# Latents of the attention scaled by 1/rms before their transposes, in a two-layer trunk on one core

## The chip, the core and the metric

The kernel runs on one core of one Trainium2 chip. A core has TensorE (PE, which also loads weights, PEld), VectorE (DVE), ScalarE (ACT), GpSimd (POOL) and SyncE (SP, which here only issues DMAs). Each takes its instructions strictly in the order of its own queue and waits on semaphores for the others. The metric is the device time of one execution in microseconds, less is better.

## What is computed

Two layers of a trunk over 256 tokens of width 1024 in fp32. Each layer is a feed forward, a mixing stage of three branches (a recurrence, a stick-breaking attention, a latent attention) and a second feed forward. The change is in the latent attention, whose queries, keys and values come from two normalized latent vectors of width 256:

```python
def rms_norm(x, g):
    xf = x.astype(jnp.float32)
    y = xf * lax.rsqrt(jnp.mean(xf * xf, axis=-1, keepdims=True) + NORM_EPS)
    return (y * g.astype(jnp.float32)).astype(x.dtype)
...
def mla_branch(c_q_raw, c_kv_raw, k_rope_raw, q_norm, w_uq, kv_norm, w_ukv, cos, sin):
    B, S, _ = c_q_raw.shape
    q = (rms_norm(c_q_raw, q_norm) @ w_uq).reshape(B, S, MLA_HEADS, MLA_NOPE + MLA_ROPE)
    q_nope, q_rope = jnp.split(q, [MLA_NOPE], axis=-1)
    q_rope = apply_rope(q_rope, cos[:, :, None, :], sin[:, :, None, :])
    kv = (rms_norm(c_kv_raw, kv_norm) @ w_ukv).reshape(B, S, MLA_HEADS, MLA_NOPE + MLA_V)
    k_nope, v = jnp.split(kv, [MLA_NOPE], axis=-1)
    k_rope = apply_rope(k_rope_raw, cos, sin)
    ...
    o = chunk_causal_softmax_attention(q, k, v, (MLA_NOPE + MLA_ROPE) ** -0.5)
```

Since 1/rms is one number per token, it can be multiplied onto the latent before `w_uq` and `w_ukv`, or onto what these give.

## The kernel before

**Weights.** All matrices come from HBM as one stream, in the order of use. Two blocks of [128, 512] make a piece. Each piece is split into two float32r parts: ACT casts it to `hi` (128x1024), DVE subtracts to get `lo`. `next_sub` asks for this two pieces ahead of PE (`AHEAD`), and there are four buffers of each part. For each block PE does pairs of matmuls, `hi` against both parts of the activations side by side (128x512) and `lo` against the high part (128x256). A whole piece is 8 such pairs. Activations are split in the same way into tiles `r`; `f` are plain fp32 tiles, `acc` and `side` tiles are PSUM.

**Groups.** The mixing stage is a list of matmul groups, `MIX_ORDER`. `cq` and `ckv` make the latents, with tokens on the partitions. `uq`, `uqr` (from the query latents), `ukv` and `uv` (from the key/value latents) have only two k-tiles; `uq` and `ukv` put features on the partitions and tokens on the free axis, `uqr` and `uv` the reverse. `rgx` and `rgg` belong to the recurrence, `q`, `k`, `v` to the stick-breaking attention, `ga`, `gb`, `gc` are gates, `bra`, `brb`, `brc` multiply the branches' results by their matrices. Of interest are these stretches of the list:

```python
v0 k0 rgx0 rgx1 k1 q0 q1 cq0 q2 q3 k2 rgx2 v1 k3 rgx3 rgg0 rgg1 rgg2 rgg3
gb0 uq0 gb1 uq1 gb2 uq2 gb3 uq3 uqr0 brb0 brb1 ckv0 brb2 brb3 ga0 ukv0 ga1 ukv1 uv0 ga2 ukv2
```

**Side work.** What isn't a group (attention of a pair of heads, the recurrence of a pair of channel blocks in `rg_chain`, latents, gelu) is written as generators. `Tasks` emits their instructions between those of the groups, each generator's in its order, where a `Clock` of estimated times says that they hold up no engine; per step only some 350 ns of side work go to PE. So the order on each queue is fixed when the program is built, by these estimates, and a change in one generator moves the others' instructions too. All that passes through `Tasks` has the line of one helper, L197, in the profile: rows are told apart by tiles.

**The latents.** `latents` evicts a latent from PSUM times 1/rms of the trunk's own norm (tile `rms`), transposes it at once (`transpose_pair`) and splits it, times the gain, into the `r` tile that `Latent` hands to the groups. Behind that, ACT sums squares (`ssc`), POOL makes 1/rms (`rc`, by `rsqrt_mean`: a multiply-add and a power), and `broadcast` turns the two columns into a row on all partitions: DVE multiplies the identity by each column, PE multiplies the diagonals by a matrix of -1, and ACT copies the result to SBUF. `head_T` then multiplies each result of `uq` and `ukv` by that row on DVE (in `scaled`), and `gen_scaled` those of `uqr` and `uv` by the columns as it evicts them.

In `rg_chain` ACT and DVE split the weights and the input of the gates of one channel pair into `r` tiles (128x512), and PE multiplies these (`side<-r,r`). There are four channel pairs.

Of the kernel before, what the change touches and what calls it, by code (L numbers as in the profile page):

```python
# [11 lines left out]
ALU = mybir.AluOpType  # L12
# [11 lines left out]
# columns of the packed per-layer vectors  # L24
# [12 lines left out]
# of each group of columns: the matrix, the first column, the k-tiles  # L37
# [9 lines left out]
def group_stream(what, n):  # L47
    """Sub-blocks of [128, 512]: one k-tile of 512 columns, or two k-tiles of 256."""
# [17 lines left out]
def layer_stream(l):  # L66
    """Order in which a layer's weight sub-blocks of [128, 512] are read."""
# [22 lines left out]
class Slots:  # L90
    """Tiles handed out in the order in which they were given back."""
# [17 lines left out]
# for each function the tables to load for it; a table holds all functions that name it  # L109
# [10 lines left out]
class Clock:  # L120
    """Estimated times (ns): until when each engine is held by what has been emitted, and
    when each tile's contents are there and have been read."""
# [33 lines left out]
class Op:  # L156
    """An instruction to be emitted, with what it costs by the clock."""
# [42 lines left out]
class Timed:  # L200
    """An engine whose instructions are emitted at once from the main stream, and left to
    the scheduler from side work."""
# [15 lines left out]
class Tasks:  # L218
    """Side work: generators whose instructions are emitted, each generator's in order, where
    the clock says that they hold up no engine. What follows a yield runs after what came  # L220
    before it has been emitted."""
# [57 lines left out]
    def advance(self, t, force=False):  # L279
        """Emits what it can of a task; whether there was any."""  # L280
# [32 lines left out]
    def drain(self, *tasks, done=None):  # L313
        """Emits the given tasks, whether they fit or not, to their end or until `done`."""
# [19 lines left out]
def trunk(tc, xT_in, pos_in, w_in, rgw_in, fin_in, const_in, out):  # L334
# [4 lines left out]
    with ctx:  # L339
# [18 lines left out]
        # x^T, two k-tiles of [128, 256] in each  # L358
# [4 lines left out]
        # [hi | lo] of two k-tiles  # L363
# [27 lines left out]
        def load(out, in_):  # L391
            """One of the first loads: they come one after the other."""
            nc.sync.dma_start(out=out, in_=in_)  # L393
            n = 4 * 128
            for d in out.shape[1:]:
                n *= d
            arrival[0] += max(n / 360, 475)
            clock.written[out.tensor.name] = (arrival[0] + 950, "dma")
# [56 lines left out]
        def both(ap):  # L455
            """[128, 256] as [128, 2, 256]"""
            return ap.rearrange("p (j t) -> p j t", j=1).to_broadcast([128, 2, 256])

        def hilo(src, hl, j=None, g=1.0):
            """src [128, 2, 256], or k-tile j of it, in two float32r parts."""  # L460
# [39 lines left out]
        def parts(a):  # L500
            """What of [128, 2, ...] each tile of a's holds."""
# [7 lines left out]
        def feature_group(kts, evac, last=0):  # L509
            """256 features of all tokens: the two halves of a bank are summed by `evac`. The  # L510
            last steps run block by block."""
# [18 lines left out]
        def token_group(kts, evac, last=0):  # L530
            """512 features, tokens on the partitions."""
# [15 lines left out]
        def narrow_group(kts, width, weights, evac):  # L547
            """The same with [128, width] weights, as (hi, lo) from `weights`."""
# [9 lines left out]
        def features(a):  # L558
            """What a feature group made, to SBUF."""
# [8 lines left out]
        def scaled(a, src, key, extra=None):  # L568
            """The same, times a scale per token."""
            f = yield from features(a)  # L570
            while key not in src:
                yield 1
# [10 lines left out]
        def transpose_pair(srcs, o):  # L583
            """Two [128, 128] blocks from column o of every token tile, to [128, 2, 256]."""
# [18 lines left out]
        def first_norm(nm, n):  # L603
            """K-tiles 2n and 2n+1 of x are final: their two parts, and squares."""
# [37 lines left out]
        def broadcast(b, r, dst, key, start=False):  # L642
            """Columns r [128, NT], to a row of them on every partition."""
# [819 lines left out]
```

## Time and profile before

| what | value |
|---|---|
| time, three runs | 1466.5, 1467.37, 1467.78 us |
| median | 1467.37 us |
| span of the profiled execution | 1467.2 us |
| PE busy | 1442.0 us (98%) |
| DVE busy | 1115.6 us (76%) |
| ACT busy | 894.3 us (61%) |
| POOL busy | 146.1 us (10%) |
| chain that ended last | PE 92%, DVE 5%, issue 1%, ACT 1% |

The span runs from the first to the last instruction of one execution; the times are of whole runs without a profiler. An engine counts as busy while one of its instructions runs, waits on a semaphore are idle. PE's matmuls overlap in the records, so the length of one row isn't what it costs: that is read from start to start. The granted clock of TensorE was 0.999 of full speed over the span.

### The profile page before, as it was taken

The numbers are of one execution on the slowest core, as the hardware profiler recorded it, in microseconds if no ns is written. First come the engines' busy times: TensorE is split into PE (matmuls) and PEld (weight loads), VectorE is DVE, ScalarE is ACT, GpSimd is POOL, SyncE is SP. The second block draws the span as 40 slices with busy tenths as digits, with TensorE's granted clock in tenths as the row PEclk, the third lists the DMA queues.
The fourth block names the chain that finished last, engine by engine and source line by source line (L and its number), as shares of the span: only waits on it lengthen the run. The fifth ranks groups of instructions, "written<-read, shape, count | busy, mean of one in ns | idle before, by whom it ended". The sixth has DMA issues, their size and how long they took to land.

```text
span 1467.2 us, 20804 instructions
## 1 busy us (share of the span) xinstructions
PE 1442.0 (98%) x8248; PEld 1261.0 (86%) x8248; DVE 1115.6 (76%) x1548; ACT 894.3 (61%) x1372; POOL 146.1 (10%) x120
## 2 busy tenths in 40 slices
PE   6999999999999999999999999999999999999998
PEld 5888888888888888888888888898888888888886
DVE  6878567689987788877677766676989877877853
ACT  4665446888665656665455554478885655566643
POOL 3000001123310000000000000111334000100001
PEclk9999999999999999999999999999999999999999
DMA  6555555534543455555545554544445434555452
GB/s 215 199 201 177 197 180 180 179 134 153 182 171 144 145 199 176 197 188 187 200 172 189 184 200 173 187 174 149 151 156 189 169 122 173 195 190 196 179 199 86
DMA packets 38081, 258.15 MB, mean 176 GB/s; under 512 B 4320, under 2 KB 4960, under 8 KB 7520
## 3 DMA queue, kind: packets, MB, share of 16 engines
q1 hardware_dynamic: 37152, 254.21, 48.5%
q0 software_dynamic: 832, 2.62, 0.6%
q8 instruction: 64, 1.05, 0.3%
q14 instruction: 33, 0.27, 0.1%
HBM read 255.77 MB, written 1.05 MB: 175 GB/s over the span
## 4 chain that ended last, share of the span: by engine, by line
PE 92%; DVE 5%; issue 1%; ACT 1%; DMA 0%; SPq 0%; POOLq 0%; POOL 0%; DVEq 0%; ACTq 0%
PE acc L197 77%; PE side L197 15%; DVE lo L197 2%; DVE f L197 2%; DVE r L197 1%; DMA x<-xT 0%; ACT hi L197 0%; ACT f L197 0%; SPq L393 0%; ACT r L197 0%; POOLq L1459 0%; POOL rms L197 0%; DVE rms L197 0%; DVEq L197 0%; ACTq L197 0%
## 5 line engine op out<-in xcount | busy, mean ns | idle before, releaser
L197 PE MATMUL acc<-r,hi 128*128 128x512 f32 x3148 | 1135.1, 403 | 9.4 <-ACT hi L197 5.5
L197 PE MATMUL acc<-r,lo 128*128 128x256 f32 x3148 | 882.7, 280 | 2.1 <-DVE lo L197 2.1
L197 DVE TENSOR_TENSOR lo<-raw,hi 128x1024 fp32r<-128x1024 f32 (+2 forms) x485 | 596.4, 1232 | 235.7 <-ACT hi L197 234.2
L197 PEld LDWEIGHTS acc<-r,hi 128*128 128x128 f32 x3148 | 593.0, 188 | 141.0 <-ACT hi L197 5.5
L197 PEld LDWEIGHTS acc<-r,lo 128*128 128x128 f32 x3148 | 596.7, 190 | 5.6 <-DVE lo L197 3.1
L197 ACT CAST hi<-raw 128x1024 fp32r<-128x1024 f32 (+2 forms) x485 | 501.5, 1040 | 137.3 <-PE acc L197 95.0
L197 POOL TENSOR_TENSOR f<-f,f 128x512 f32<-128x512 f32 (+1 forms) x51 | 89.1, 1753 | 1039.8 <-ACT f L197 955.8
L197 ACT COPY f<-acc 128x512 f32<-128x512 f32 x166 | 97.4, 587 | 126.7 <-PE acc L197 122.9
L197 ACT ACTIVATE f<-f 128x256 f32<-128x256 f32 (+3 forms) x190 | 94.9, 502 | 84.5 <-DVE f L197 83.3
L197 DVE TENSOR_TENSOR f<-acc,f 128x512 f32<-128x512 f32 x166 | 113.8, 685 | 39.1 <-ACT f L197 38.5
L197 DVE TENSOR_TENSOR f<-f,f 128x512 f32<-128x512 f32 x179 | 126.3, 706 | 8.8 <-ACT f L197 2.6
L197 PE MATMUL acc<-hi,r 128*128 128x512 f32 (+2 forms) x344 | 96.9, 358 | 0.0
L197 ACT CAST r<-f 128x256 fp32r<-128x256 f32 (+2 forms) x130 | 58.6, 455 | 61.1 <-DVE f L197 59.8
L197 PE MATMUL side<-r,hi 128*128 128x512 f32 x260 | 92.0, 395 | 0.0
L197 PE MATMUL side<-r,lo 128*128 128x256 f32 x260 | 72.6, 279 | 0.0
L197 PE MATMUL side<-f,f 128*128 128x256 f32 (+1 forms) x320 | 71.6, 327 | 0.0
L197 PEld LDWEIGHTS acc<-hi,r 128*128 128x128 f32 x344 | 61.6, 189 | 8.4
L197 DVE TENSOR_TENSOR r<-f,r 128x256 fp32r<-128x256 f32 (+2 forms) x130 | 64.7, 502 | 2.0 <-ACT r L197 1.9
L197 PE MATMUL acc<-lo,r 128*128 128x512 f32 (+2 forms) x172 | 61.1, 355 | 0.0
L197 PEld LDWEIGHTS side<-r,hi 128*128 128x128 f32 x260 | 48.7, 187 | 11.1
L197 PEld LDWEIGHTS side<-f,f 128*128 128x128 f32 x320 | 45.8, 190 | 4.9
L197 PEld LDWEIGHTS side<-r,lo 128*128 128x128 f32 x260 | 49.1, 189 | 0.0
(89 smaller groups left out, 806.2 us busy)
## 6 DMA issues: line engine op xcount, KB each, us to landing
raw<-w SPq DMA_DIRECT2D x238, 1024.0 KB, 4.8
f<-rgw POOLq DMA_DIRECT2D x8, 256.0 KB, 3.4
raw<-w SPq DMA_DIRECT2D x7, 256.0 KB, 6.9
out<-f SPq DMA_DIRECT2D x4, 256.0 KB, 2.2
x<-xT SPq DMA_DIRECT2D x3, 256.0 KB, 6.7
f<-fin POOLq DMA_DIRECT2D x2, 256.0 KB, 3.7
cst<-const SPq DMA_DIRECT2D x1, 336.0 KB, 5.5
x<-xT SPq DMA_DIRECT2D x2, 128.0 KB, 2.5
```

The costliest lines, as they stand in the source:

```text
L197: return self.f(*self.args, **self.kw)
```

## The change

The squares, the mean and the power of a latent now come before its transposes, and DVE multiplies the two token tiles of the latent by 1/rms in place, in SBUF. What `uq`, `uqr`, `ukv` and `uv` give is then normalized already: `head_T` skips the product, `gen_scaled` copies, and the broadcast of the row is gone, with the tiles that held it. Comments and docstrings are dropped as well.

```diff
         def scaled(a, src, key, extra=None):
             f = yield from features(a)
+            if key is None:
+                return f
             while key not in src:
                 yield 1
             rb = both(src[key])
...
-        def broadcast(b, r, dst, key, start=False):
+        def broadcast(b, r, dst, key):
...
-            pe.matmul(b[:, 256:512], neg_one, d[:, 0:256], start=start, stop=True, skip_group_check=True)
+            pe.matmul(b[:, 256:512], neg_one, d[:, 0:256], start=False, stop=True, skip_group_check=True)
...
-        def gen_scaled(a, scales):
+        def gen_scaled(a, scales=None):
             o = []
             for t in range(NT):
                 f = yield from FT.take()
-                if t == 0:
+                if scales is None:
+                    act.copy(f, bank_of(a, t)) if t == 0 else dve.tensor_copy(f, bank_of(a, t))
+                elif t == 0:
                     act.activation(out=f, in_=bank_of(a, t), func=AF.Copy, scale=scales[t])
...
             def run(a):
-                f = yield from scaled(a, mx["nm"] if r == "rb" else mx, r, extra)
+                f = yield from scaled(a, mx["nm"], r, extra)
...
                 yield
                 acc.give(a)
                 cs_ = [c[:, t * 256:(t + 1) * 256] for t in range(NT)]
+                junk = yield from FT.take()
+                for t in range(NT):
+                    act.activation(out=junk[:, 0:256], in_=cs_[t], func=AF.Square, accum_out=mx["ssc"][:, i, t:t + 1])
+                yield
+                FT.give(junk)
+                rsqrt_mean(mx["rc"][:, i], mx["ssc"][:, i], 256)
+                for t in range(NT):
+                    dve.tensor_scalar(cs_[t], cs_[t], mx["rc"][:, i, t:t + 1], None, op0=ALU.mult)
                 yield
                 b = yield from transpose_pair(cs_, 0)
                 hl = yield from RT.take()
...
                 side.give(b)
+                FT.give(c)
                 mx["cT"][i] = hl
-                yield
-                junk = yield from FT.take()
-                for t in range(NT):
-                    act.activation(out=junk[:, 0:256], in_=cs_[t], func=AF.Square, accum_out=mx["ssc"][:, i, t:t + 1])
-                yield
-                FT.give(junk, c)
-                rsqrt_mean(mx["rc"][:, i], mx["ssc"][:, i], 256)
-                yield
-                b = yield from side.take()
-                yield from broadcast(b, mx["rc"][:, i], mx, ("rbq", "rbkv")[i], start=True)
                 if i == 1:
                     yield from k_rope(mx, f)
...
                 elif what == "uq":
-                    feature_group(Latent(0), head_T(mx, "qn", n, "rbq"))
+                    feature_group(Latent(0), head_T(mx, "qn", n, None))
...
                 elif what == "ukv":
-                    feature_group(Latent(1), head_T(mx, "kn", n, "rbkv"))
+                    feature_group(Latent(1), head_T(mx, "kn", n, None))
                 elif what == "uv":
-                    token_group(Latent(1), head_v(mx, "v_ml", n, mx["rkv"]))
+                    token_group(Latent(1), head_v(mx, "v_ml", n, None))
```

The order of the built program shows where instructions land. Numbers behind a tile's name tell buffers apart and differ between the two programs.

DVE, first layer, around the key/value latents, before: the eviction of the latent (`f_120<-acc_84,rms`), the two low parts behind the transposes (`r_100<-side_87,cst`), and the diagonals made from `rc`.

```order
L197 TENSOR_SCALAR f_120<-acc_84,rms_171 128x256
L197 SCALAR_TENSOR_TENSOR f_113<-f_122,f_133 128x256 x2
L197 TENSOR_TENSOR lo<-raw,hi 128x1024
L197 SCALAR_TENSOR_TENSOR r_100<-side_87,cst,r_100 128x256
L197 TENSOR_TENSOR f_110<-f_125,cs 128x8x32
L197 SCALAR_TENSOR_TENSOR f_119<-f_132,f_119 128x512
L197 SCALAR_TENSOR_TENSOR r_100<-side_87,cst,r_100 128x256
L197 TENSOR_TENSOR f_110<-f_110,f_138 128x8x32
L197 TENSOR_TENSOR lo<-raw,hi 128x1024
L197 TENSOR_SCALAR f_118<-cst,rc_1815 128x128 x2
L197 TENSOR_TENSOR f_115<-acc_85,f_115 128x512
```

The same place now: the latent is `f_139`, the low parts are `r_98<-side_89,cst`.

```order
L197 TENSOR_SCALAR f_139<-acc_84,rms_171 128x256
L197 SCALAR_TENSOR_TENSOR f_126<-f_122,f_126 128x512
L197 TENSOR_TENSOR f_137<-f_137,f_121 128x8x32
L197 TENSOR_TENSOR lo<-raw,hi 128x1024
L197 SCALAR_TENSOR_TENSOR r_93<-f_111,r_93 128x2x256
L197 TENSOR_SCALAR f_139<-f_139,rc_1815 128x256 x2
L197 SCALAR_TENSOR_TENSOR f_127<-f_122,f_126 128x256 x2
L197 TENSOR_TENSOR lo<-raw,hi 128x1024
L197 SCALAR_TENSOR_TENSOR r_98<-side_89,cst,r_98 128x256
L197 TENSOR_TENSOR f_128<-acc_85,f_128 128x512
L197 SCALAR_TENSOR_TENSOR f_128<-f_138,f_128 128x512
L197 SCALAR_TENSOR_TENSOR r_98<-side_89,cst,r_98 128x256
```

The scalings (`f_139<-f_139,rc`) stand ahead of the low parts, and the two diagonals behind them are gone. Behind the last row come the key's rotation (14 instructions of 128x32 and 128x64) and two weight splits. On POOL four products of 128x512 stand directly ahead of `rc`, and the product behind it reads the scans `f_127`.

DVE, first layer, before, where the splits of the third and fourth channel pair end (`r_98` of the third, `r_103` and `r_93` of the fourth).

```order
L197 TENSOR_TENSOR lo<-raw,hi 128x1024
L197 TENSOR_TENSOR f_119<-acc_84,f_119 128x512
L197 TENSOR_TENSOR f_119<-f_119,f_109 128x512
L197 SCALAR_TENSOR_TENSOR f_128<-f_126,f_127 128x256
L197 TENSOR_TENSOR r_98<-f_116,r_98 128x512
L197 TENSOR_TENSOR lo<-raw,hi 128x1024
L197 TENSOR_TENSOR r_103<-f_117,r_103 128x512
L197 TENSOR_TENSOR r_93<-f_118,r_93 128x512
L197 TENSOR_TENSOR r_94<-side_86,r_94 128x2x256
```

And now, some 24 rows earlier, the third pair's (`r_104`, `r_93`), and 21 and 27 rows later, in the second fence, the fourth pair's (`r_103`, `r_96`).

```order
L197 TENSOR_TENSOR lo<-raw,hi 128x1024
L197 SCALAR_TENSOR_TENSOR f_128<-f_126,f_127 128x256
L197 TENSOR_TENSOR r_101<-f_135,r_101 128x384
L197 SCALAR_TENSOR_TENSOR f_128<-f_126,f_127 128x256
L197 TENSOR_TENSOR r_104<-f_138,r_104 128x512
L197 TENSOR_TENSOR r_93<-f_112,r_93 128x512
L197 TENSOR_TENSOR lo<-raw,hi 128x1024
```

```order
L197 TENSOR_TENSOR r_103<-f_141,r_103 128x512
L197 TENSOR_TENSOR lo<-raw,hi 128x1024
L197 TENSOR_TENSOR f_138<-acc_84,f_138 128x512
L197 TENSOR_TENSOR f_138<-f_138,f_109 128x512
L197 TENSOR_TENSOR f_112<-side_86,f_112 128x256
L197 TENSOR_TENSOR lo<-raw,hi 128x1024
L197 TENSOR_TENSOR f_112<-side_89,f_112 128x256
L197 TENSOR_TENSOR r_96<-f_130,r_96 128x512
```

What stood in one run is now in two places, 46 rows and more apart.

ACT, first layer, now, between the gates of the third pair and the scores of a stick-breaking head (`f_113`); the rows from one cast of weights to the second after it.

```order
L197 CAST hi<-raw 128x1024
L197 CAST r_94<-side_86 128x2x256
L197 CAST r_98<-f_117 128x384
L132 ACT_TABLE_LOAD
L197 ACTIVATE f_116<-side_87,cst 128x256
L197 ACTIVATE f_114<-side_87,cst 128x256
L197 ACTIVATE f_115<-f_116,tiny,s_77 128x256
L197 ACTIVATE f_113<-side_88 128x384
L132 ACT_TABLE_LOAD
L197 ACTIVATE f_113<-f_113 128x384
L197 CAST hi<-raw 128x1024
L197 COPY f_139<-acc_84 128x512
```

Behind these follow one more `ACTIVATE f_113<-f_113`, a third table load, one `ACTIVATE f_116<-side_86,cst` and the next cast of weights. The number of table loads in the whole program is 33 in both.

## Rows read from the trace of the kernel before

**Rows 1.** The page: span, PE's busy time, the chain that ended last by engine.

```profile
span 1467.2 us, 20804 instructions
...
PE 1442.0 (98%) x8248; PEld 1261.0 (86%) x8248; DVE 1115.6 (76%) x1548; ACT 894.3 (61%) x1372; POOL 146.1 (10%) x120
...
PE 92%; DVE 5%; issue 1%; ACT 1%; DMA 0%; SPq 0%; POOLq 0%; POOL 0%; DVEq 0%; ACTq 0%
```

**Rows 2.** Waits of PE: who waited for whom, us in total, times, longest.

```profile
PE side L197 <- DVE r L197: 4.7, 4, 1.5
...
PE side L197 <- DVE f L197: 1.9, 2, 0.9
```

**Rows 3.** Timeline of PE at the gates: start, length, instruction, idle before.

```profile
340.48 0.38 PE L197 MATMUL side<-r,r 128*128 128x256 f32 x1 [0.90 <-DVE r L197]
...
344.32 0.62 PE L197 MATMUL side<-r,r 128*128 128x256 f32 x3 [1.47 <-DVE r L197]
```

**Rows 4.** Timeline of DVE and POOL at the same moments.

```profile
340.35 1.63 DVE L197 TENSOR_TENSOR lo<-raw,hi 128x1024 fp32r<-128x1024 f32 x1
341.90 2.37 DVE L197 TENSOR_TENSOR r<-f,r 128x512 fp32r<-128x512 f32 x2
...
340.99 2.13 POOL L197 TENSOR_TENSOR f<-f,f 128x512 f32<-128x512 f32 x1
```

**Rows 5.** Timeline of PE around the broadcast of the query latents, first layer.

```profile
268.36 0.39 PE L197 MATMUL acc<-r,hi 128*128 128x512 f32 x1
...
268.71 0.39 PE L197 MATMUL acc<-r,hi 128*128 128x512 f32 x1
...
269.05 0.59 PE L197 MATMUL side<-f,cst 128*128 128x256 f32 x2
...
269.83 0.40 PE L197 MATMUL acc<-r,hi 128*128 128x512 f32 x1
```

**Rows 6.** Timeline of POOL, DVE and PE around the broadcast of the key/value latents.

```profile
404.18 0.19 POOL L197 TENSOR_SCALAR rc<-ssc 128x2 f32<-128x2 f32 x1 [10.85 <-ACT f L197]
404.45 0.72 POOL L197 TENSOR_TENSOR rc<-rc,nhalf 128x2 f32<-128x2 f32 x1
...
405.15 2.28 POOL L197 TENSOR_TENSOR f<-f,f 128x512 f32<-128x512 f32 x1
...
406.21 1.83 DVE L197 TENSOR_SCALAR f<-cst,rc 128x128 f32<-128x128 f32 x2
...
408.10 0.70 PE L197 MATMUL side<-f,cst 128*128 128x256 f32 x2 [0.93 <-DVE f L197]
```

**Rows 7.** Instructions on the tile `rc`: shortest, median and longest, in ns.

```profile
L197 DVE TENSOR_SCALAR f<-cst,rc x8: 278/444/1772, 267.2 to 1129.8; 128x128 f32<-128x128 f32 x8
```

**Rows 8.** Groups by shape, PE and DVE: count, busy us, mean ns, idle before.

```profile
L197 PE MATMUL side<-f,cst 128*128 128x256 f32 x20 | 6.1, 388 | 1.9 <-DVE f L197 1.9
...
L197 DVE TENSOR_TENSOR lo<-raw,hi 128x1024 fp32r<-128x1024 f32 x476 | 590.4, 1242 | 232.5 <-ACT hi L197 230.9 <-PE side L197 0.3
L197 DVE TENSOR_TENSOR f<-f,f 128x512 f32<-128x512 f32 x171 | 122.9, 719 | 8.6 <-ACT f L197 2.6
...
L197 DVE TENSOR_TENSOR_SCAN f<-f,f 128x256 f32<-128x256 f32 x16 | 11.3, 723 | 0.0
...
L197 DVE TENSOR_TENSOR r<-f,r 128x512 fp32r<-128x512 f32 x22 | 16.8, 780 | 0.0
...
L197 DVE TENSOR_SCALAR f<-f,sm 128x256 f32<-128x256 f32 x16 | 5.5, 346 | 0.0
...
L197 DVE TENSOR_TENSOR f<-f,cs 128x32 f32<-128x32 f32 x16 | 2.0, 184 | 0.0
```

**Rows 9.** Groups by shape, ACT.

```profile
L197 ACT CAST hi<-raw 128x1024 fp32r<-128x1024 f32 x476 | 497.0, 1049 | 133.7 <-PE acc L197 95.0 <-PE side L197 25.7 <-issue 7.3
...
L132 ACT ACT_TABLE_LOAD x33 | 42.3, 1283 | 1.3 <-PEq L1455 0.7
...
L197 ACT ACTIVATE f<-side,cst 128x256 f32<-128x256 f32 x32 | 14.6, 474 | 6.2 <-PE side L197 6.1
```

More of the change, by code (lines that the diff above doesn't have):

```diff
@@ L1014, in run @@
             def run(a):
-                qs = yield from gen_scaled(a, mx["rq"])
+                qs = yield from gen_scaled(a)
                 yield
@@ L1149, in mix @@
             mx["rc"] = pool.tile([128, 2, NT], F32, name=f"rc{l}")
-            mx["rq"] = [mx["rc"][:, 0, t:t + 1] for t in range(NT)]
-            mx["rkv"] = [mx["rc"][:, 1, t:t + 1] for t in range(NT)]
             mx["sm"] = pool.tile([128, 3, HEADS, NT], F32, name=f"sm{l}")
@@ L1292, in mix @@
                     RT.give(*nm["xT"].values())
-            FT.give(nm["rb tile"], mx["rbq tile"], mx["rbkv tile"])
+            FT.give(nm["rb tile"])
             FT.give(mx["kr"])
```

## The prediction

> **What bounds the kernel now.** I read the page's head first: of a span of 1467.2 us TensorE (PE) is busy for 1442.0 us, 98%, and the chain that ended last lies on PE for 92% and on VectorE (DVE) for 5% [rows 1]. So work taken from DVE, ScalarE (ACT) or GpSimd (POOL) is worth nothing by itself. Worth something are only PE's own instructions and the moments at which PE stands still.
>
> Those moments are in the list of what PE waited for [rows 2]. Two kinds lie in the mixing stage: waits of `side` matmuls for DVE's `r` tiles, 4.7 us in 4 times, and for DVE's `f` tiles, 1.9 us in 2 times. They come at the same places in both layers, half of them in each. PE's other idle time is nearly all at the kernel's start, which the change doesn't touch.
>
> The timeline of the first layer tells what they are. At 340.48 and 344.32 us gate matmuls of the recurrence (`side<-r,r`) waited 0.90 and 1.47 us for the low part of their input [rows 3]. DVE wasn't idle then but behind: it had a weight split and two such splits in a row, and while POOL worked on a product of 2.13 us the weight split took 1.63 us and the two others together 2.37 us [rows 4]; by the means of their kinds that would be 1.24 and 1.56 us [rows 8]. The wait for an `f` tile is the row of 1/rms of the key/value latents: the broadcast matmul at 408.10 stood in PE's queue 0.93 us for the diagonals that DVE makes from `rc`, and the two instructions that make them took 1.83 us [rows 6].
>
> **The change, part by part.** *PE loses four fp32 matmuls*, one broadcast per latent and layer; they are 8 of the 20 records `side<-f,cst` of 128x256 [rows 8], each matmul being recorded as two. Their price is read where one stood with no wait: from 268.71 to 269.83 PE did two pairs of weight matmuls (high and low part) and one broadcast in 1.12 us, and the pair before them took 0.35 us, 268.36 to 268.71 [rows 5]. So 1.12 - 0.70 = 0.42 us each, 4 x 0.42 = 1.7 us. Nothing covers these, PE being the chain.
>
> *The wait ahead of the key/value broadcast goes with it*: 1.9 us for both layers [rows 2].
>
> *DVE loses* 16 products of 128x512 (`f<-f,f`, 8 per layer) of 0.72 us [rows 8] and 8 diagonal instructions of 0.44 us in the median [rows 7], and gets 8 scalings of 128x256 inside SBUF. The trace has that operation and shape on another tile, `f<-f,sm`, at 0.35 us [rows 8]. That is 11.5 + 3.5 - 2.8 = 12 us less. The six copies that replace a scaling per token out of PSUM cost about what those did, and ACT loses four copies of the broadcast. I price all this at nothing: PE's 98% covers it, and if DVE were the bound where these stood, it would be up to 12 us, of which the trace shows no more than the waits already named. Squares, mean and power are as many as before, only ahead of the transposes.
>
> *What moves.* The scheduler decides by estimated times, so from the first latent on nearly every side instruction stands elsewhere. The order shows what becomes of the 4.7 us. Before, the last low splits of the third and fourth channel pair stood together on DVE with one weight split between them. Now the third pair's two come some 25 rows earlier, and the fourth pair's stand two weight splits apart and some 25 rows later. The pile for which PE waited is gone, and I take the whole 4.7 us off. Its bounds are that and nothing, if the pile has only moved.
>
> *What the moves may add.* Two places look tight in the new order, each once per layer.
>
> First, the key/value latents. Behind the last ckv matmul DVE has up to the weight split that follows the scalings: two weight splits of 1.24 us, a product of 0.72, the two scalings of 0.35, two scans of 0.72 [rows 8], together 5.3 us, and an eviction, a rotation and a split of about 0.5 us each, so 7 us. Then come the two low parts of the latents, an eviction with its product and the key's rotation in 14 instructions of some 0.18 us [rows 8], another 5 us, and only then the weight split that PE needs four weight pieces after ckv. A piece is 8 pairs of 0.35 us, so 11.2 us, and a dozen transposes add about 1.3 us. That split is done after 7 + 5 + 1.2 = 13.2 us and wanted after 12.5: 0.7 us late. Should POOL hold DVE up once more, as at 406.21, where 1.83 us went into two instructions that take 0.28 us at best [rows 6, 7], it is 1.3 us more, 2.0 in all. The least is nothing.
>
> Second, ACT has three table loads close together, with a single cast of weights among them. Up to the second cast that is 3 x 1.28 for the loads, 2 x 1.04 for the casts and ten smaller instructions of about half a us [rows 9], 11 us for two pieces, while PE uses up two pieces in 5.6 us. The weights are split two pieces ahead, 5.6 us of lead. The two amounts are nearly equal; I take 0.8 us late, with bounds of nothing and of 2.8 us, if the lead was one piece only.
>
> Together 2 x (0.7 + 0.8) = 3.0 us, between nothing and 2 x (2.0 + 2.8) = 9.6 us. That the latents are ready later costs nothing by itself: twelve groups of matmuls lie between cq and its first use, and brb2, brb3 and ga0 between ckv and its own.
>
> **The sum** against the profiled span: 1467.2 - 1.7 - 1.9 - 4.7 + 3.0 = 1461.9 us. The median of the three runs, 1467.4, is 0.2 us above that span, so 1462 us.
>
> **A row against the change.** The diagonal's instructions, with one input and both ends in SBUF as the new scalings have them, took 0.28 us at least, 0.44 in the median and 1.77 at most, all of one shape [rows 7]; the slow pair ran while POOL multiplied for 2.28 us [rows 6]. So the change keeps the exposure that made the broadcast late. If POOL multiplies at one scaling of each latent, it costs DVE 4 x (1.83 - 2 x 0.28) = 5 us, and the sum is 1467 us if PE waits for all of it.
> The Trainium skill's page "SBUF — State Buffer", section "Who interferes with whom", says that such an instruction of VectorE and one of GpSimd exclude each other on a shared pair of ports for its whole length, so that the second to issue waits; the trace agrees at 406.21.
> I don't add these 5 us, since for the key/value latents POOL's next product reads the scans that DVE makes behind the scalings and can't run beside them; it is a rival.
>
> **The rivals.** A time is told from the 1467.4 us of before when it differs by more than 0.2%, 2.9 us: under 1464.4 or over 1470.3.
> *No new waits*: 8.3 us gained, 1459 us. For it speaks that PE shows hardly a wait at the other tight places of the old order; against it the two sums above. 20%.
> *The waits come back elsewhere*: the two tight places cost over 5.5 us in all, or a gate pile re-forms: 1466 us, no change. For it speaks that DVE and ACT are still full there. 17%.
> *POOL holds up the scalings*, as worked out above: 1467 us, no change. For it speaks the pair at 406.21, against it what POOL's next product reads. 6%.
> *Slower*: POOL is late with the power. In the new order four products of 128x512, of 2.1 to 2.3 us each in the rows seen [rows 4, 6], stand on POOL right ahead of the mean and the power, where it was idle for 10.85 us before [rows 6]. If they start only when ckv ends, the power is there 4 x 2.1 + 0.9 = 9.3 us behind it. DVE, which takes its instructions in order and is there after some 3.5 us, stands still for 5.8 us with the weight splits queued behind, and PE waits for those: 2 x 5.8 us on top of the forecast, 1473 us. It decides from 4.2 us per layer, a power 7.7 us behind ckv. Against it: most of the four products have their inputs some pieces earlier. 5%.
> *The forecast*: 52%.
>
> **Numbers.** 1462 us. The range runs from no new waits, 1458.5, to waits that come back nearly whole, 1467.0. Faster 0.71 (nearly all of the forecast and of no new waits), same 0.24, slower 0.05.
>
> **What would show it.** Right: 12 records `side<-f,cst` of 128x256 are left, PE's list has no wait for an `f` tile in the mixing stage and under 1 us per layer for `r` tiles; DVE is busy some 12 us less and PE some 1.7 us less. Wrong: PE waits of over 2 us per layer for `lo` behind ckv, for `hi` near the three loads, or for the latents' transposes with POOL named behind DVE. The forecast falls too if the gate splits are late again, now for the third pair alone, which would return 2 to 5 us.

## The result, and the profile after

The changed kernel takes 1477.96 us (1477.45 to 1479.15, four runs) against 1466.93 us (1466.5 to 1467.78, four runs) of the kernel before: a ratio of 1.0077, 95% interval 1.0064 to 1.009. It is slower by 11 us, where 5 us less were forecast. The profiled execution took 1478.08 us, its span is 1476.3.

The page of the changed kernel: span, busy time by engine, the chain that ended last.

```profile
span 1476.3 us, 20770 instructions
...
PE 1448.3 (98%) x8240; PEld 1260.0 (85%) x8240; DVE 1103.8 (75%) x1532; ACT 892.3 (60%) x1368; POOL 143.1 (10%) x120
...
PE 85%; DVE 6%; ACT 3%; POOL 2%; issue 2%; DMA 0%; SPq 0%; POOLq 0%; DVEq 0%; ACTq 0%
```

Against [rows 1], DVE is busy 11.8 us less and PE has 8 records less, as worked out. But PE's busy time grew by 6.3 us with less work in it, and PE's share of the last chain fell from 92 to 85%, with DVE, ACT and POOL in its place.

What PE waited for, in the whole execution:

```profile
PE acc L197 <- DVE r L197: 5.8, 3, 2.0
PE side L197 <- DVE f L197: 5.6, 8, 1.2
PE acc L197 <- ACT hi L197: 5.5, 1, 5.5
PE acc L197 <- DVE lo L197: 2.7, 2, 2.5
PE side L197 <- DVE r L197: 1.2, 2, 0.6
```

The two rows of `hi` and `lo` and 1.8 us of the first are the kernel's start. The rest is 4.0 + 5.6 + 1.2 = 10.8 us, all in the mixing stages, where [rows 2] had 4.7 + 1.9 = 6.6. The waits of gate matmuls (`side<-r,r`) are gone. The new places, PE's timeline in the first layer (the second has the same six, 1235.05 for the last):

```profile
340.37 0.44 PE L197 MATMUL side<-r,tri_r 128*128 128x384 f32 x1 [0.58 <-DVE r L197]
...
354.58 0.50 PE L197 MATMUL side<-r,hi 128*128 128x512 f32 x1 [0.22 <-DVE f L197]
...
356.05 0.50 PE L197 MATMUL side<-r,hi 128*128 128x512 f32 x1 [0.85 <-DVE f L197]
...
374.17 0.50 PE L197 MATMUL side<-hi,r 128*128 128x512 f32 x1 [1.23 <-DVE f L197]
...
403.32 0.81 PE L197 MATMUL side<-cst,f 128*128 128x128 f32 x4 [0.53 <-DVE f L197]
...
508.43 0.47 PE L197 MATMUL acc<-r,hi 128*128 128x512 f32 x1 [2.01 <-DVE r L197]
```

They are, in order: a stick-breaking head's scores; two `uq` groups and the `uqr` group, which need a PSUM tile `side` that the eviction hasn't given back; the transposes of the key/value latents, which now wait for the scalings; and `brc0`, which waits for the last pair of attention heads.

How 354.58 and 356.05 come about can be followed over three engines. POOL, ACT and DVE in the changed kernel:

```profile
342.94 2.20 POOL L197 TENSOR_TENSOR f<-f,f 128x512 f32<-128x512 f32 x1 [1.48 <-DVE f L197]
...
350.50 1.29 POOL L197 TENSOR_TENSOR f<-f,f 128x512 f32<-128x512 f32 x1
...
345.17 0.63 ACT L197 ACTIVATE r<-f 128x512 fp32r<-128x512 f32 x1 [2.48 <-POOL f L197]
345.81 1.28 ACT L132 ACT_TABLE_LOAD   x1
347.10 0.63 ACT L197 ACTIVATE f<-f 128x512 f32<-128x512 f32 x1
347.64 1.03 ACT L197 CAST hi<-raw 128x1024 fp32r<-128x1024 f32 x1
...
348.71 1.22 DVE L197 TENSOR_TENSOR lo<-raw,hi 128x1024 fp32r<-128x1024 f32 x1 [3.02 <-ACT hi L197]
350.65 2.21 DVE L197 TENSOR_TENSOR lo<-raw,hi 128x1024 fp32r<-128x1024 f32 x1 [0.72 <-ACT hi L197]
...
354.11 0.42 DVE L197 TENSOR_TENSOR f<-side,f 128x256 f32<-128x256 f32 x1
...
355.58 0.41 DVE L197 TENSOR_TENSOR f<-side,f 128x256 f32<-128x256 f32 x1
```

ACT stands 2.48 us behind a product of POOL, then loads a table, and the next cast of weights is late; DVE idles 3.02 us for that cast, and the evictions of `uq` (`f<-side,f`) stand behind the late splits. So DVE is the engine named at PE, and it is the last of three that were late; POOL's product had itself waited 1.48 us for an earlier result of DVE. Neither the scalings nor `rc` are in these rows.

The wait at 403.32 is another matter. There DVE stood still for `rc`, and the scalings behind it are what the transposes waited for:

```profile
402.91 0.62 DVE L197 TENSOR_SCALAR f<-f,rc 128x256 f32<-128x256 f32 x2 [0.62 <-POOL rc L197]
```

This is the only one of the six waits that ends at an operation that the change moved or added, 2 x 0.53 us of the 10.8.

**The pace.** The waits don't explain PE's longer busy time. PE in fixed stretches of steady weight stream: us, busy time, matmuls, granted clock, DMA share, GB/s. Kernel before:

```profile
790.00:890.00 100.00, 100.00 (x568) 1.00 0.52 186
1330.00:1380.00 50.00, 50.00 (x291) 1.00 0.53 191
```

Changed kernel:

```profile
620.00:720.00 100.00, 100.00 (x579) 1.00 0.54 190
790.00:890.00 100.00, 100.00 (x568) 1.00 0.53 190
1330.00:1380.00 50.00, 50.00 (x285) 1.00 0.52 186
```

In these feed-forward stages PE does nothing but pairs of one 128x512 and one 128x256 matmul, never waits, and has the full granted clock. Yet it does 579 matmuls in 100 us in one stage and 568 in another, with nothing between: from start to start a pair takes 346.7 or 353.3 ns. The kernel before had the slower pace in one feed-forward stage of four, the changed kernel in two, and also from 508 to 556 us and from 1235 to 1300.

Add up all steps from one matmul's start to the next, in both kernels. A kind of step is given by the two matmuls' tiles and shapes, and each step is held against the fastest tenth of its kind. The 9.1 us between the spans are then, to within 0.1 us: steps late by under 30 ns (the pace) 5.4, by over 240 ns behind the start (waits and the restart behind each) 5.1, by something in between (shorter stops) 0.9, the kernel's first 60 us -1.6, and what steps there are -0.6, the four matmuls included. If the matmul before also counts for the kind, the two large terms stay (5.5 and 5.2), but shorter stops are 1.5 and the last term is -1.4, so the small terms aren't firm.

### The profile page after: what moved, and what is told of

It is laid out like the page before. It is cut to its first block, busy times and chain, and to the rows that moved or that the text cites. A ratio compares the mean times of both kernels' runs of the same rounds, so it can differ in the third digit from the quotient of the medians.

```text
span 1476.3 us, 20770 instructions
## 1 busy us (share of the span) xinstructions
PE 1448.3 (98%) x8240; PEld 1260.0 (85%) x8240; DVE 1103.8 (75%) x1532; ACT 892.3 (60%) x1368; POOL 143.1 (10%) x120
## 4 chain that ended last, share of the span: by engine, by line
PE 85%; DVE 6%; ACT 3%; POOL 2%; issue 2%; DMA 0%; SPq 0%; POOLq 0%; DVEq 0%; ACTq 0%
PE acc L197 72%; PE side L197 13%; DVE lo L197 3%; POOL f L197 2%; DVE f L197 2%; ACT f L197 1%; ACT hi L197 1%; DVE r L197 1%; ACT L132 1%; DMA raw<-w 0%; ACT r L197 0%; POOL rc L197 0%; SPq L393 0%; DVE sm L197 0%; POOLq L1460 0%
## 5 line engine op out<-in xcount | busy, mean ns | idle before, releaser
L197 DVE TENSOR_TENSOR f<-f,f 128x512 f32<-128x512 f32 (+1 forms) x163 | 114.2, 701 | 8.3 <-ACT f L197 2.6
```

The lines of the kernel that those rows point to most:

```text
L197: return self.f(*self.args, **self.kw)
```

## The experiments

Two theories. **Order**: the scheduler's estimates put the side instructions elsewhere, and PE waits at other places; what was multiplied where has no part in it. **Late operations**: squares, mean, power and scalings ahead of the transposes are what PE ends up waiting for. A third question is the pace. In the table, waits are PE's in the mixing stages of the profiled execution, the same sum as above; the last column counts its matmuls in the stretches 620 to 720, 790 to 890 and 1330 to 1380 us (fast pace: 579, 579, 290; slow: 568, 568, 285).

| kernel | time, us | ratio to before, interval | waits, us | matmuls |
|---|---|---|---|---|
| before | 1467 | 1 | 6.6 | 579, 568, 291 |
| changed | 1478.0 | 1.0064 to 1.009 | 10.8 | 579, 568, 285 |
| q_only | 1481.9 | 1.0075 to 1.011 | 15.4 | 579, 568, 290 |
| kv_only | 1468.2 | 0.9993 to 1.0012 | 7.3 | 579, 568, 291 |
| before_cross150 | 1492.9 | 1.016 to 1.0199 | 21.5 | 579, 567, 285 |
| before_side500 | 1464.5 | 0.9971 to 0.999 | 2.9 | 579, 569, 291 |
| before_slack300 | 1483.8 | 1.0102 to 1.0132 | 15.5 | 569, 579, 290 |
| before_c110_d100 | 1466.8 | 0.9989 to 1.0006 | 1.0 | 568, 579, 285 |
| after_slack300 | 1459.1 | 0.993 to 0.996 | 0 | 579, 579, 285 |
| after_pool39 | 1463.8 | 0.9965 to 0.9985 | 4.3 | 579, 568, 290 |
| after_bra3 | 1469.6 | 1.0007 to 1.0025 | 7.4 | 579, 569, 290 |
| after_nudges | 1477.6 (one run) | | 11.2 | 578, 576, 289 |
| after_nudge1 | 1472.5 | 1.0019 to 1.0074 | 11.5 | 579, 579, 290 |
| before_nudge1 | 1464.2 | 0.9968 to 0.9987 | 6.6 | 578, 579, 290 |
| after_slack300_nudge | 1460.5 | 0.9939 to 0.9972 | 0 | 568, 579, 291 |
| after_slack300_n12 | 1460.9 | 0.9945 to 0.9973 | 0 | 579, 571, 285 |

**One latent alone.** In `latents` the new lines run for one `i` only, and the other latent keeps its broadcast:

```diff
+                early = i in EARLY_SCALE        # (0,) or (1,)
+                if early:
                     junk = yield from FT.take()
```

> Only the query latent is scaled ahead of its transposes; the key/value latent is as before. Theory of order: the loss of 11 us comes from where the estimated clock puts the side instructions (waits of PE at other places, 5 us in all) and from TensorE's pace (346.7 or 353.3 ns for a pair of weight matmuls, 5.5 us in all), and not from the moved operations. Then this half has a list of waits of its own, in both layers at the same places, and the two halves' differences to before don't add up to +11 us. Theory of late operations: squares, mean, power and scalings ahead of the transposes are what PE ends up waiting for, each latent for its own. Then the key/value half, which shows 0.53 us of such a wait per layer and loses a broadcast, comes out at about 1465 to 1468 us, and this half carries the rest, 1474 to 1478 us, with the sum of the two differences at +11.

> Only the key/value latent is scaled ahead of its transposes; the query latent is as before. Theory of order: waits at places of its own, and the difference to before together with that of the query half is not +11 us. Theory of late operations: 1465 to 1468 us, with the wait ahead of the key/value transposes (0.53 us per layer) as the only new one.

The query half alone comes out slower than the changed kernel, the key/value half changes nothing: +14.7 and +1.0 us by the medians. By the medians the query half misses the 1474 to 1478 us that late operations expected, and the sum is 15.7 and not 11. Both decide less than it seems: one of the four times of the query half is 1478.15, and by their intervals the two differences are 11 to 16 and -1 to 2 us. The lists of waits say more. Those of the query half are at the places of the changed kernel (0.60, 0.22, 0.85, 1.51 and 2.01 us at 340.8, 355.0, 356.5, 374.6 and 511.8), and there is one more: its key/value broadcast, no operation of the change, waits 2.60 us, where [rows 6] had 0.93.

```profile
407.43 1.22 PE L200 MATMUL side<-f,cst 128*128 128x256 f32 x2 [2.60 <-DVE f L200]
```

So the new waits come with the order that the query latent's change brings, some 80 us and more behind that latent (it is scaled at 263.2), and not from any work of the change at these places. The key/value half keeps the waits at the gates and has the 0.53 us ahead of its transposes, as expected, but two more of 0.26 and 0.53 us per layer at 411.0 and 411.8, which late operations had not foreseen.

A part of the query half's loss isn't waiting. In its profile the granted clock is at the lower of its two levels (1.2 of 2.4 GHz) in two stretches, each beside a wait of PE of over 2 us (2.60 and 2.01), the first of them here:

```profile
407.10:410.40 3.30, 2.97 (x9) 0.50 0.00 0
```

A pair takes 640 ns there. Held against the medians of the same steps in the kernel before and the changed one, the two stretches cost some 3.3 us, an estimate for this execution. The profile of the changed kernel has the same wait of 2.01 us and no such stretch.

**The kernel before in another order.** Nothing is computed otherwise; one constant of the scheduler's estimate changes.

```diff
-    CROSS = 130
+    CROSS = 150          # before_cross150
-    SIDE = 350
+    SIDE = 500           # before_side500
-    SLACK = 50
+    SLACK = 300          # before_slack300
-            self.cost = 68 + rate * n
+            self.cost = 100 + rate * n    # before_c110_d100, with CROSS = 110
```

> The kernel before, computing the same with the same instructions; only the scheduler's estimate of the delay between two engines is 150 ns and no longer 130, which moves side instructions from the middle of the first layer on. Theory of order: the time moves by 2 us or more, up or down, with PE's waits at other places and perhaps another pace in some stage. Theory of late operations: nothing was made late, so 1466 to 1468 us.

> The kernel before, with the same instructions, but the scheduler may put 500 ns of side matmuls between two weight steps and no longer 350. Theory of order: the time moves by 2 us or more, either way; if the waits at the gates (4.7 us) and at the key/value broadcast (1.9 us) go, down to about 1461 us. Theory of late operations: no change, 1466 to 1468 us.

> The kernel before with the same limit of 300 ns that took 19 us off the changed kernel. If a limit of 300 ns is simply the better rule, it gains here too, down to about 1458 to 1462 us, the waits at the gates and at the broadcast gone. If every order has its own places to wait and the 50 ns just fitted the kernel before, as 300 ns fit the changed one, the waits come up elsewhere and the time is 1470 us or more.

The kernel before, waits of PE with an estimated delay of 150 ns between engines:

```profile
PE acc L197 <- DVE r L197: 6.8, 3, 2.9
PE side L197 <- DVE r L197: 6.7, 5, 2.5
PE side L197 <- DVE f L197: 6.1, 5, 1.9
...
PE side L197 <- ACT r L197: 4.2, 2, 2.1
```

20 ns in an estimate cost 26 us, more than twice what the change cost; 500 ns of side work gained 3.0 us, with the waits at the gates and at the broadcast gone and 2.9 us of others in their place; and the limit of 300 ns cost 16. These are moves of order alone. The late operations can't explain any of them.

Of the 26 us, too, a part is the clock. The profile with 150 ns has five stretches at the lower level in the mixing stages, some 24 us in all, each beside or just behind waits of PE. The longest, which follows a wait of 2.08 us, and the full clock behind it, then two starts from within the longest:

```profile
1086.60:1096.70 10.10, 9.16 (x28) 0.50 0.01 2
1098.00:1106.00 8.00, 8.00 (x48) 1.00 0.37 131
```

```profile
1094.94 0.63 PE L197 MATMUL acc<-r,hi 128*128 128x512 f32 x1
...
1095.58 0.63 PE L197 MATMUL acc<-r,hi 128*128 128x512 f32 x1
```

By the medians as above the five cost some 9 us in this execution (an estimate). Not every long wait is followed by such a stretch: those of 1.98 us at 517.5 and 1.88 us at 1131.0 aren't, that of 1.98 us at 1253.7 is. before_slack300 has two (some 3 us), at its two waits of 5.12 us. So a wait can cost more than its length.

**The changed kernel in another order.**

```diff
-    SLACK = 50
+    SLACK = 300          # after_slack300
-            self.cost = 150 + (166 if kw.get("op") == ALU.pow else 2.1) * n
+            self.cost = 150 + (166 if kw.get("op") == ALU.pow else 3.9) * n    # after_pool39
-ga3 ukv3 bra0 bra1 uv1 gc0 bra2 gc1 gc2 gc3 brc0 brc1 brc2 brc3 bra3 out0 out1 out2 out3
+ga3 ukv3 bra0 bra1 uv1 gc0 bra2 gc1 gc2 gc3 bra3 brc0 brc1 brc2 brc3 out0 out1 out2 out3    # after_bra3
```

> The changed kernel, with the same instructions, but the scheduler may put a side instruction into a queue when by its estimate it would hold the engine up by 300 ns and no longer 50. Theory of order: the waits of PE in the mixing stages, 12.8 us in the changed kernel, stand elsewhere and have another sum; 1458 to 1470 us, clearly under the 1478 of the changed kernel. Theory of late operations: the same squares, power and scalings stand ahead of the same transposes, so 1474 us or more.

The list of after_slack300, complete:

```profile
PE acc L197 <- ACT hi L197: 5.6, 1, 5.6
PE acc L197 <- DVE r L197: 3.0, 2, 2.8
PE acc L197 <- DVE lo L197: 2.1, 2, 1.9
```

All of it is the kernel's start. (The expectation's 12.8 us should read 10.8.) The changed kernel, with every operation in it, runs PE through both mixing stages without a wait, at 1459.1 us: 8 us under the kernel before, 19 under the changed kernel. The same limit cost the kernel before 16 us. So neither limit is the better one; each order has its own.

> The changed kernel; only the scheduler's estimate of a GpSimd product of 128x512 is 2.15 us, as its trace has them (2.19 to 2.21), and not 1.23. If ScalarE's queue, held up 2.5 us by such a product at 342.7, is behind PE's waits of 0.22, 0.85 and 1.23 us at 354.6, 356.1 and 374.2, these three go in both layers, 4.6 us in all: 1473 us. By the theory of order other waits may come up in their place; by the theory of late operations nothing changes, 1476 to 1479 us.

The three waits behind POOL's product went, as expected, and so did the one at `brc0`. Those for the scaled key/value latents grew, to 1.20 and 1.65 us. There the timeline of POOL and DVE in after_pool39 shows what the prediction had as a rival:

```profile
400.51 1.74 POOL L197 TENSOR_TENSOR f<-f,f 128x512 f32<-128x512 f32 x1
...
401.05 1.96 DVE L197 TENSOR_SCALAR f<-f,rc 128x256 f32<-128x256 f32 x2
```

The two scalings took 1.96 us beside a product, against 0.62 us in the changed kernel. The time fell further than to the 1473 us, by the wait at `brc0` and by the faster pace in the last stage. That the three waits went is what the chain through POOL's product asks for; but this order differs from the changed kernel's at many places, so the run alone doesn't tell that cause from another order's luck.

> The changed kernel with the fourth group of the recurrent branch's product ahead of the first of the latent attention's, instead of behind the last, so that the last pair of attention heads has one group, some 11 us, more time. If the wait of 2.0 us per layer at 508.4 and 1235.1 is only the last pair's lateness, it goes: 4.0 us, 1474 us, if no later stage changes its pace. If the attention as a whole is behind, a part of the wait stays.

The wait at `brc0` is gone in both layers, and the other five are at the places where they were, one of them longer (`uqr`, 1.51 for 1.23 us): the last pair of heads was late, by less than one group. The time fell by 8.3 us and not 4. By steps as above the waits gave 3.8 us and the pace 4.8: the stretches behind `brc0` in both layers and the last feed-forward stage (290 for 285) ran at the faster pace without being touched.

**The pace.** A nudge is one matmul more, ahead of a hidden group's first, which overwrites it; the scheduler doesn't count it, so nothing else moves.

```diff
+                if nudge and i == 0:
+                    nc.tensor.matmul(bank_of(a, 0)[:, 0:nudge], wh[:, 0:128], hl[:, 0:nudge], start=True, stop=False, skip_group_check=True)
                 for b in range(2):
                     for j, h, hl, vh, vl in held:
```

> The changed kernel with 24 extra small matmuls on PE, six in each feed-forward stage, of 32, 64, 96, 128, 192 and 256 columns, each ahead of a group whose first matmul overwrites it; the order of everything else is the same. If the pace of the weight stream is a state that PE falls into where its stream is broken, it changes from 346.7 to 353.3 ns per pair or back at some of the 24. If the pace belongs to the weights or tiles of a stage, each stage keeps its own: 346.7 in both of the first layer, 353.3 in both of the second.

From the distances of starts, some 20 pairs on each side of a nudge, the same in all four stages:

```
columns   pace before   pace behind   stages
 32       346.7         346.7         4 of 4
 64       346.7         346.7         4 of 4
 96       346.7         353.3         4 of 4
128       353.3         346.7         4 of 4
192       346.7         353.3         4 of 4
256       353.3         346.7         4 of 4
```

So the pace doesn't belong to weights, tiles or load: it is a state of the stream, which one small matmul can set either way. It seems to go by the width, but each width stood ahead of the same hidden group in every stage and met only the one pace of its row: what 32, 64, 96 or 192 columns do to the slower pace isn't shown. By steps as above the pace took 5.5 us off, but the extra matmuls, the breaks around them and one stretch at the lower granted clock behind the wait at `brc0` (some 1.6 us, an estimate) gave it back: 1477.6 us in the one run.

> The changed kernel with one matmul more, 128 columns wide, ahead of the third hidden group of the second layer's first feed-forward stage; nothing else is moved. If the pace is a state: that stage goes from 353.3 to 346.7 ns per pair, some 290 pairs, 1.9 us; and if the last feed-forward stage comes out fast too, as it did with the 24 small matmuls, another 1.7 us: 1474 to 1476 us. If another engine bounds these stages, the time stays within 0.5 us of the changed kernel.

> The kernel before with the same one matmul more. If the pace is a state: 1.9 us less, 1465 us, with the last feed-forward stage as it was, or 1467 us if that one falls into the slower pace. If another engine bounds the stage: no change.

The second layer's first feed-forward stage, with and without the one matmul, in the changed kernel (the kernel before has the same two counts):

```profile
755.00:905.00 150.00, 150.00 (x851) 1.00 0.53 191
```

```profile
755.00:905.00 150.00, 150.00 (x868) 1.00 0.54 195
```

The first is without, the second with it. By the medians, one matmul of 0.06 us took 5.5 us off the changed kernel and 3.4 off the kernel before. The second is clear of noise; of the changed kernel's five times four are within 0.4 us of each other and one is 1483.08, so that there the counts of matmuls are the better evidence. I had counted 290 pairs; with the down projection the stage has some 500, and 500 x 6.7 ns = 3.3 us. In the changed kernel the last stage came out fast as well.

> The changed kernel with the hold-up limit of 300 ns and one matmul of 128 columns more ahead of the third hidden group of the last feed-forward stage, which ran at 353.3 ns per pair there. If the pace is a state: 320 pairs at 346.7, 2.1 us less than the 1459.1 without the extra matmul, 1457 us. If not: 1459 us.

> The changed kernel with the limit of 300 ns and twelve small matmuls more, three in each feed-forward stage ahead of the third, ninth and fifteenth hidden group: 128 columns in the first stage of each layer, 256 in the second. So far such a matmul ended the slower pace in all 9 cases where it met it; how it acts on the faster pace has not been seen. If it always leaves the faster pace behind, the four stages run at 346.7 ns per pair in this execution and in the others, and the time is 1457 us with less scatter than the 2 to 3 us of the last two kernels. If it turns the faster pace into the slower, stretches between two of them are slow and the time is 1459 to 1462 us.

The last stage of after_slack300_nudge did turn fast (285 to 291). But its second feed-forward stage ran slow, 568 for 579, although the program is the same up to there. So the pace isn't fixed by the program, and one profile, or one median, has some of it by chance; that a small difference in time from the kernel's start sets it is a guess. Until then 128 or 256 columns had met the slow pace eleven times (the expectation miscounts) and always ended it. Of the twelve nudges, 128 columns turned fast into slow three times and slow into fast twice, and left the fast pace behind a stretch of both; 256 kept the fast pace three times, ended the slow one once and kept it twice. A nudge is a toggle with a rule that these runs don't give, and no cure: 1460.5 us with one, 1460.9 with twelve, where 1457 had been expected of both.

> The kernel before with the same instructions and other estimates: 110 ns and not 130 between engines, 100 ns and not 68 for a VectorE instruction's fixed part. By the theory of order the kernel before, too, has an order with hardly a wait of PE in the mixing stages: 1459 to 1462 us, and what the change is worth by itself is the difference between two such orders, its four matmuls of 0.42 us, 1.7 us. If the changed operations were worth more than these matmuls, the changed kernel with its best order (1459 us) keeps 4 us or more over this one.

The order has 1.0 us of waits, as expected, yet the time is that of the kernel before and not 1459 to 1462 us: by steps as above waits and restarts are 6.1 us less, and the slow pace, in two stages instead of one (568 and 285), takes back 5.3. So what the change is worth by itself isn't settled: between the two orders nearly free of waits lie 7.7 us, but by steps as above the one of before has 3.9 us more of pace, 1.7 of waits with their restarts and 2.9 of short stops (PE changes between weight stream and side work 428 times in it, 404 in after_slack300). That is more than the whole difference, and the kernel before with the limit of 300 ns also changes 404 times, so the stops go with the order; the four matmuls' 1.7 us can't be read out of it.

## Why the prediction was wrong

By its steps, the failed ones last.

*The four matmuls, 1.7 us*: gone, 12 records are left. Nothing shows another price. *DVE 12 us less, worth nothing by itself*: 11.8 us less, as worked out; no run shows that it is worth anything. The scalings took 0.35 us each in the changed kernel (346 to 354 ns), as priced. *POOL at the scalings* (6%) didn't come in the changed kernel, but did in after_pool39 with another order, for 1.3 us. *POOL late with the power* (5%) was the right mechanism at a tenth of its price: DVE idled 0.62 us per layer for `rc`, where 5.8 had been worked out.

*The broadcast's wait, 1.9 us*: gone, but the key/value transposes wait 0.53 us per layer in its place. The first tight place had 0.7 us there, for a weight split that comes too late; PE didn't wait for a split at all. That the sizes are near each other is luck.

*The gates' waits, 4.7 us, taken off whole*: `side<-r,r` waits no more, as the order showed.

*The second tight place, ACT's three table loads, 0.8 us per layer*: it cost nothing. The three loads are at these times in the changed kernel:

```profile
317.41 1.28 ACT L132 ACT_TABLE_LOAD   x1
...
321.19 1.28 ACT L132 ACT_TABLE_LOAD   x1
...
324.87 1.28 ACT L132 ACT_TABLE_LOAD   x1
```

```profile
323.98 1.23 DVE L197 TENSOR_TENSOR lo<-raw,hi 128x1024 fp32r<-128x1024 f32 x1 [4.11 <-ACT hi L197]
```

DVE idled 4.11 us for the cast between them, so ACT was late as worked out, but PE has no wait before 340.37 there: the weights split ahead covered it. The waits of `uq`, 1.07 us per layer, come some 30 us later and from POOL's product.

**The step that failed** is "what the moves may add", 3.0 us from two places, with 9.6 as its most. I went through the order around the latents and took the rest for granted ("PE shows hardly a wait at the other tight places of the old order"). Five of the six waits are at other places: 0.58 at the scores, 0.22 and 0.85 at `uq`, 1.23 at `uqr`, 2.01 at `brc0`, the last 100 us behind the key/value latents; 4.9 us per layer, 9.8 in both. None of the three long waits that were named as signs of being wrong came. The forecast had the waits fall from 6.6 to 3.0 us; they rose to 10.8. That is 7.8 us of the 14.4 by which the span missed (1476.3 for 1461.9). And the chances: with an order redrawn from the first latent on, "slower" had 5% for one mechanism, while the runs of order alone above spread from -3 to +26 us. What counted was less the change than the new order that came with it.

**What was missing** is the pace, about 5.4 us between the two profiles, for which the sum had no term. That it is a state that a matmul can set is shown; that the changed kernel fell into the slow one for longer because of its changed stream is likely, since its four times agree to 0.1%, but isn't shown, and the run in which a stage flipped by itself says that chance has a part.

Of the kernels run, the fastest is the changed kernel with `SLACK = 300`: 1459.1 us, 0.4 to 0.7% under the kernel before.

## What to carry to other kernels

Where a program is laid out by estimates, a change of arithmetic is measured together with a new order, and the order can be worth several times the change: before judging it, run both in a few orders, and let the estimates be perturbed without the change to see how far that alone moves the time. In the trace go by the waits over the whole stage and not only near the edit, and follow each one back until an engine waits for nothing: the engine named at the end may be the third in a row. Look at the granted clock behind each long wait, since a stretch at the lower level cost some 1 to 4 us more in these runs. And when a busy engine grows busier with less work, count its instructions in equal windows before looking for waits.

## What the runs showed of the hardware

A stream of 128x512 and 128x256 float32r matmuls, each with its own weights, has two paces at one granted clock of 1.00, the higher level, 346.7 and 353.3 ns per pair, and keeps either for hundreds of pairs; a single matmul of 96 or 192 columns in between ended the faster pace (4 of 4 each), one of 128 or 256 the slower in 14 of 16 cases, one of 32 or 64 left the faster as it was (8 of 8). What the state consists of isn't settled. The Trainium skill, "TensorE: Matmul & The Clock Gate", section "Back-to-back issue gap", gives N / 2.4 + 2.5 ns as the isolated gap from one matmul to the next at the higher level; an estimate from it is 325 ns for such a pair, with one pace. The trace has 7 to 9% more and two of them. For a stream in which each matmul has its own weight load the same section of the Trainium skill says that this formula is too high at large N and puts 131 ns at N = 512; the 512-column matmuls here take 230 ns and more from their start to the next. The scheduler's estimate of PE is the formula of the isolated gap, and so runs ahead of PE.

A POOL product of 128x512 that started 0.16 us behind a DVE weight split took 2.20 us (342.94), and a split that started 0.15 us behind a product took 2.21 us (350.65), where the two took 1.29 (350.50) and 1.22 us (348.71) unhindered. The Trainium skill, "SBUF — State Buffer", section "Who interferes with whom", says that a DVE instruction with two inputs in SBUF and a POOL instruction that reads SBUF contend, and that the one issued first holds up the other: the trace agrees, in both directions.

In four of the runs the granted clock fell to the lower level within a mixing stage, each time beside or just behind a wait of PE of about 2 us or more (2.60 us at 407.4 in q_only, 5.12 at 348.4 in before_slack300), and a pair took 640 ns there instead of 346.7 or 353.3. Waits of the same length also passed without it, as the 2.01 and 2.00 us at `brc0` in the changed kernel's profile.
